# Output projection: half 0 left open in eight banks, mix loaded into its final places, factors loaded ahead of values

## The chip, the cores and the metric

One core of a Trainium2 chip runs the whole program. The metric is device time in microseconds (us), the median of the runs shown below. Every matrix product works on numbers split in two (a rounded high part and the rest), so that one fp32 product takes three matmuls: high x high, high x low, low x high.

## The reference

One layer of a hybrid decoder: for a prompt of 2048 rows and 32 sample rows, of width 1024. Cut to what matters here:

```python
def _layer_prompt(x, biases, ...):
    q, k, v, u, vg = _project(x, norm1_g, w_in)          # rmsnorm(x) @ w_in
    for (w, d), bias_hj in zip(BRANCHES, biases):        # (128,1), (512,4), (2048,16)
        o, l = _dilated_prompt(q, k, v, bias_hj, d, w // d + 1)
        outs.append(o); lses.append(l)
    att = _merge_branches(outs, lses)                    # softmax over the branches' lse
    gate = _spatial_gate(vn, sgu_w, sgu_b)
    x = x + jnp.concatenate([att, u * gate], axis=-1) @ w_out
    return x + _swiglu(x, norm2_g, w_gate, w_up, w_down)
```

The product with `w_out` (1024 x 1024) is the output projection, and its left operand is called mix here: 512 columns of attention (8 heads of 64) and 512 of the gating unit.

## The kernel before

**Stages.** Projection of the input and the gating unit come first; then attention, head by head; then, for each of two blocks of 1024 rows, output projection, norm, gate and up products, down products and the final norm. Block 0 is rows 0 to 1023 in 8 tiles of 128. Block 1 is the other 8 tiles and the sample rows.

**Attention.** Each of 8 heads is 20 items of softmax work. A planner holds the code: `at(step, phase, fn)` puts a function at a step (one item, about 2.2 us) and a phase of it, and the code of each engine is written in that order. `L` is the step of the last item and `U0` is `L + 7`, where attention's last pieces end. The branches of a head are merged with factors: `weights_store` (L957) writes them from ACT's queue to `f_d` in DRAM, `merge_load` reads them back, spread over partitions, `merge` multiplies and adds in three operations on POOL or DVE, and `merge_store` writes a head pair's attention columns to `cat_d` in DRAM, where mix lies transposed. Attention's rows lie there in two parts that are added later. Heads are worked in pairs; a slice of mix is 128 of its 1024 columns, and slice s = 7 holds heads 6 and 7, the last to be ready. Merges of a head run during the next head's items; those of head 7 are left for the output projection.

**Output projection.** A unit is one tile of 128 rows by one half of 512 output columns: 8 slices x 3 matmuls into one bank (`out_unit`, L1255 to L1257), followed by an add of the bank to `acc`, which holds x. `load_cat` brings a tile of mix from `cat_d` to a staging tile `fr` (two buffers, used by the weights' `load_wo` too) and the second part of attention to `raw`. `split_cat` adds the two on DVE, copies the sum to the high part `xh` on ACT (L122) and subtracts for the low part `xl` on DVE (L125). A weight goes through `fr` likewise: ACT makes `woh` or `wol` from it, POOL subtracts. All these loads, x (`acc`), factors of head 7 and stores of its merges share SP's queue, which issues in order and waits where an entry must wait.

**Order in block 0.** At steps U0 to U0+7, units of half 0 run without slice 7 (21 matmuls each), are added to `acc`, and head 7 is merged meanwhile: factors from step U0+2 on, chunk by chunk of 512 rows. `last_load` (L1401) and `last_split` bring slice 7. From step U0+8 on, each step holds a whole unit of half 1 and slice 7 of a half 0 unit (3 matmuls), which is added to `acc` in turn. Unit 0 takes its mix from `pair` tiles filled in attention's last steps.

**Order in block 1.** A plain loop: tile i+1 is split ahead of unit i, tile i+3 is loaded, and the weights of half 1 are loaded at tiles 1 to 4.

Of the kernel before, what the change touches and what calls it, by code (L numbers as in the profile page):

```python
# [10 lines left out]
F32 = mybir.dt.float32  # L11
# [8 lines left out]
P = 128  # L20
# [44 lines left out]
def hymba_step(ctx: ExitStack, tc: tile.TileContext, A: dict, O: dict):  # L65
# [896 lines left out]
    def merge_load(h, ch):  # L962
        if h < H - 1:
            f = pair_tile(F32)
            mf[h, ch] = (f[:, 0], f[:, 1])
            act.dma_start(f, dap(f_d, h * 2 * T + ch * 512, [[0, P], [T, 2], [1, 512]]))
# [145 lines left out]
    def fraw():  # L1112
        return pool_["fw"].tile([P, 1024], F32, name="fr", tag="fr", bufs=2)

    def fminor():
        return raw_tile()

# [72 lines left out]
    def load_acc(B, i):  # L1190
        if B.rows[i] == P:
            B.acc[i] = fc.tile([P, D], F32, name="acc%d" % i, tag="acc%d" % i)
# [22 lines left out]


    def load_cat(B, i, ns, staged=None):
        t0 = (B.b0 + i) * P
        if staged is None:
            r = fraw().rearrange("p (s t) -> p s t", s=KD)  # L1220
            parts = (r[:, 0:4], r[:, 4:8])
            m = fminor().rearrange("p (s t) -> p s t", s=4)
        else:
            r = None
            *parts, m = (x.rearrange("p (s t) -> p s t", s=4) for x in staged)
        na = ns - 4
        raws["c", B.b0 + i] = (r, parts, m)
        for dst, r0, n in ((parts[0], 0, 4), (parts[1], DA, na), (m, D, na)) if staged else ((r, 0, ns), (m, D, na)):
            sync.dma_start(dst[:, 0:n], cat_d[r0:r0 + n * P, t0:t0 + P].rearrange("(s p) t -> p s t", p=P))

    def split_cat(B, i, ns, place, eng=dve):
        r, parts, m = raws.pop(("c", B.b0 + i))
        ch, cl = B.cat[i] = place
        na = ns - 4
        eng.tensor_add(parts[1][:, 0:na], parts[1][:, 0:na], m[:, 0:na])
        if r is not None:
            split_sb(ch[:, 0:ns], cl[:, 0:ns], r[:, 0:ns], eng_lo=eng)
        else:
            split_sb(ch[:, 0:4], cl[:, 0:4], parts[0], eng_lo=eng)
            split_sb(ch[:, 4:ns], cl[:, 4:ns], parts[1][:, 0:na], eng_lo=eng)  # L1240

    def place_of(B, i):

        return B.xh[:, :, i * P:(i + 1) * P], B.xl[:, :, i * P:(i + 1) * P]

    def out_unit(B, i, half, ss=range(KD)):
        tick()
        hs = slice(half * 512, (half + 1) * 512)
        ps = ps_o()
        for s in ss:  # L1250
            first, last = s == ss[0], s == ss[-1]
            wh, wl = B.wo[half, s]
            if B.rows[i] == P:
                ch, cl = (x[:, s, :] for x in B.cat[i])
                pe.matmul(ps, ch, wh, start=first, stop=False)  # L1255
                pe.matmul(ps, ch, wl, start=False, stop=False)  # L1256
                pe.matmul(ps, cl, wh, start=False, stop=last)  # L1257
            else:
                c = cats[:, (s + 4) % KD, :]
                pe.matmul(ps[0:2 * SR], c, wh, start=first, stop=False)  # L1260
                pe.matmul(ps[0:2 * SR], c, wl, start=False, stop=last)
        if B.rows[i] == P:
            dve.tensor_add(B.acc[i][:, hs], B.acc[i][:, hs], ps)
        else:
            tmp = zn_tile()[0:SR]
            act.activation(tmp, ps[SR:2 * SR, :], AF.Copy)
            dve.tensor_add(B.acc[i][0:SR, hs], B.acc[i][0:SR, hs], ps[0:SR])
            dve.tensor_add(B.acc[i][0:SR, hs], B.acc[i][0:SR, hs], tmp)

    def rms_b(s1, n):  # L1270
# [123 lines left out]

    last = {}

    def last_load(ch):

        x, m = last[ch] = (fraw(), None)
        for z, r0 in enumerate((DA + 3 * P, D + 3 * P)):  # L1400
            sync.dma_start(x[:, z * 512:(z + 1) * 512], cat_d[r0:r0 + P, ch * 512:(ch + 1) * 512])  # L1401

    def last_split(ch):
        x = last.pop(ch)[0]
        dve.tensor_add(x[:, 0:512], x[:, 0:512], x[:, 512:1024])
        if ch == 0:
            ch_, cl_ = B.cat[0]
            split_sb(ch_[:, 7], cl_[:, 7], x[:, 0:P], eng_lo=dve)
            split_sb(B.xh[:, 7, P:512], B.xl[:, 7, P:512], x[:, P:512], eng_lo=dve)
        else:  # L1410
            split_sb(B.xh[:, 7, 512:1024], B.xl[:, 7, 512:1024], x[:, 0:512], eng_lo=dve)

# [21 lines left out]
    B.xl = fc.tile([P, KD, TB], F32R, name="xl2", tag="xl2")  # L1434
    for i in range(1, 3):
        load_cat(B, i, 7)
    for i in range(2):
        load_acc(B, i)
    for nm in ("norm2_g", "final_g"):
        gain.append(row_tile(nm))  # L1440
    for i in range(1, 8):
        at(U0 + i - 1, "early", lambda i=i: split_cat(B, i, 7, place_of(B, i)))
        if i + 2 < 8:
            at(U0 + i - 1, "early", load_cat, B, i + 2, 7)
        if i > 1:
            at(U0 + i - 2, "misc", load_acc, B, i)
    h = H - 1
    for ch, s, eng in ((0, 3, dve), (1, 3, pool), (2, 5, dve), (3, 5, pool)):
        at(U0 + s - 1, "misc", merge_load, h, ch)
        at(U0 + s, "misc", merge, h, ch, eng)  # L1450
        at(U0 + s + 1, "misc", merge_store, h, ch, ch + 1)
    at(U0 + 6, "misc", lambda: [sync.dma_start(g_, dap(A[nm], 0, [[0, P], [1, D]])) for g_, nm in zip(gain, ("norm2_g", "final_g"))])
    for ch in range(2):
        at(U0 + 7 + ch, "misc", last_load, ch)
        at(U0 + 8 + ch, "early", last_split, ch)
    for s2, s, e in ((0, 3, 4), (1, 4, 5), (2, 5, 6), (3, 6, 7)):
        at(U0 + s, "misc", load_wo, B, 1, s2, fraw)
        at(U0 + e, "misc", half1_split, B, s2)
    for i in range(8):
        at(U0 + i, "values", out_unit, B, i, 0, range(7))  # L1460
        at(U0 + 8 + i, "values", out_unit, B, i, 1)
        at(U0 + 8 + i, "values", out_unit, B, i, 0, (7,))
        at(U0 + 8 + i, "out", lambda i=i: later(1, norm2_a, B, i))
    at(U0 + 10, "misc", load_gate, 0)
    at(U0 + 12, "misc", split_gate, 0)
    plan.run(10 ** 9)

    for bi, B in enumerate(blocks):
        if bi:
            for i in range(B.nt):  # L1470
                if i + 1 < B.nt:
                    split_cat(B, i + 1, 8, place_of(B, i + 1))
                if i + 3 < B.nt:
                    load_cat(B, i + 3, 8)
                elif i + 3 < B.nt + 2:
                    pass
                out_unit(B, i, 0)
# [20 lines left out]
        for f in range(NF):  # L1498
# [32 lines left out]
            if f % FC == FC - 1:  # L1531
# [4 lines left out]
                elif end:  # L1536
                    nb.xh = fc.tile([P, KD, TB], F32R, name="xh2", tag="xh2")
                    nb.xl = fc.tile([P, KD, TB], F32R, name="xl2", tag="xl2")
                    for n, fn, args in ((1, load_wo, (nb, 0, 2, fraw)), (1, load_cat, (nb, 0, 8)),
                                        (3, split_wo, (nb, 0, 2, gate_tiles, dve)), (3, load_wo, (nb, 0, 3, fraw)),  # L1540
                                        (4, split_cat, (nb, 0, 8, place_of(nb, 0))), (4, load_cat, (nb, 1, 8)),
                                        (5, split_wo, (nb, 0, 3, gate_tiles, dve)), (5, load_cat, (nb, 2, 8))):
                        later(n, fn, *args)
# [113 lines left out]
```

## Time and profile before

| | us |
|---|---|
| median of 3 runs | 2867.06 (2865.78 to 2869.12) |
| the profiled execution | 2874.03 |
| its span, first to last instruction | 2872.2 |
| block 0's output projection, first matmul to the first of the gate | 1059.31 to 1184.51 |
| block 1's, first matmul to the end of half 1's first unit | 1934.45 to 2013.66 |

The mean granted TensorE clock was 0.963 of full. The page cuts the span into 40 equal slices of 71.8 us, and each digit is the busy share of TensorE in one, in tenths:

```profile
PE   8988897988998987999999999997999999999997
```

Block 0's output projection lies in slices 15 to 17 (8, 7, 9), block 1's in 27 to 29 (9, 7, 9). Under a row of a timeline, the bracket holds the idle time just before the instruction and what ended it. "SPq" and "ACTq" are DMA issues.

### The profile page before, as it was taken

What the parts mean: (1) busy time and instruction counts of PE and PEld (TensorE: products, weight loads), DVE (VectorE), ACT (ScalarE), POOL (GpSimd) and SP (SyncE); (2) the same over time, 40 slices, a digit from 0 to 9 for tenths busy, and PEclk for the clock granted to TensorE, in tenths of its full rate; (3) what the DMA queues carried; (4) which work ended last, traced back from release to release, by engine and by line L of the source; (5) the groups of instructions that cost most, each with busy time, mean ns of one, the idle gap of its engine ahead of it and who ended that gap; (6) DMA issues with size and microseconds to landing.
All of it is one profiled execution on the core that took longest, in us unless ns stands there. A gap on an engine that the chain in (4) does not pass through costs nothing.

```text
span 2872.2 us, 33608 instructions
## 1 busy us (share of the span) xinstructions
PE 2680.6 (93%) x13058; PEld 2260.2 (79%) x13058; DVE 1197.0 (42%) x2287; ACT 762.5 (27%) x1426; POOL 849.5 (30%) x558
## 2 busy tenths in 40 slices
PE   8988897988998987999999999997999999999997
PEld 6776675667888875888888888875799999999996
DVE  3257775335677764522222222244522222222224
ACT  5413233435676751310100000021300000000002
POOL 1034742121243442232232222211132222222222
PEclk9999998999899988999999999998999999999999
DMA  8654933676556556232223222235132222222211
GB/s 243 206 176 128 283 105 111 185 217 227 154 174 197 150 163 189 88 112 93 88 89 110 95 88 88 95 107 181 54 108 88 88 88 88 88 88 88 89 44 61
DMA packets 285940, 367.44 MB, mean 128 GB/s; under 512 B 18487, under 2 KB 214248, under 8 KB 279764
## 3 DMA queue, kind: packets, MB, share of 16 engines
q1 hardware_dynamic: 270868, 341.56, 37.2%
q10 hardware_dynamic: 14912, 23.73, 3.3%
q8 instruction: 103, 1.69, 0.3%
q14 instruction: 57, 0.47, 0.1%
HBM read 309.88 MB, written 125.47 MB: 152 GB/s over the span
## 4 chain that ended last, share of the span: by engine, by line
PE 71%; DVE 8%; DMA 6%; ACT 4%; issue 4%; POOL 2%; SPq 1%; ACTq 0%; POOLq 0%; DVEq 0%
PE ps_o L1341 17%; PE ps_s L1315 12%; PE ps_s L1316 12%; PE ps_s L1317 12%; PE ps_s L295 2%; PE ps_s L296 2%; PE ps_s L297 2%; DVE pl L847 1%; PE ps_o L1255 1%; PE ps_o L1257 1%; PE ps_o L1256 1%; PE ps_s L810 1%; DMA fr<-in_w_out_dram 1%; PE ps_o L861 1%; PE ps_t L838 1%
## 5 line engine op out<-in xcount | busy, mean ns | idle before, releaser
L1315 PE MATMUL ps_s<-xh,gh 128*128 128x352 f32 (+1 forms) x1760 | 624.1, 355 | 0.0
L1317 PE MATMUL ps_s<-xh,gl 128*128 128x352 f32 (+1 forms) x1760 | 620.2, 352 | 0.0
L1316 PE MATMUL ps_s<-xl,gh 128*128 128x352 f32 (+1 forms) x1760 | 619.5, 352 | 0.0
L1341 PE MATMUL ps_o<-dw,hw 128*128 128x512 f32 x2112 | 499.8, 397 | 9.7 <-DVE acc L1343 9.7
L1341 PEld LDWEIGHTS ps_o<-dw,hw 128*128 128x128 f32 x2112 | 395.6, 188 | 109.0 <-DVE acc L1343 15.6
L1319 ACT ACTIVATE zn<-ps_s 128x352 f32<-128x352 f32 (+1 forms) x110 | 57.1, 519 | 1319.0 <-PE ps_s L1317 1319.0
L1320 DVE TENSOR_TENSOR zn<-zn,ps_s 128x352 f32<-128x352 f32 (+1 forms) x110 | 64.6, 587 | 721.5 <-ACT zn L1319 721.5
L1315 PEld LDWEIGHTS ps_s<-xh,gh 128*128 128x128 f32 x1760 | 332.3, 189 | 33.5
L1316 PEld LDWEIGHTS ps_s<-xl,gh 128*128 128x128 f32 x1760 | 331.3, 188 | 31.6
L1317 PEld LDWEIGHTS ps_s<-xh,gl 128*128 128x128 f32 x1760 | 330.4, 188 | 32.4
L1343 DVE TENSOR_TENSOR acc<-acc,ps_o 128x512 f32<-128x512 f32 x352 | 241.1, 687 | 214.4 <-PE ps_o L1341 214.4
L125 POOL TENSOR_TENSOR hw<-zn,hw 128x512 fp32r<-128x512 f32 (+2 forms) x110 | 119.8, 1089 | 661.1 <-DVE hw L124 592.9
L125 POOL TENSOR_TENSOR gl<-fr,gh 128x1024 fp32r<-128x1024 f32 x88 | 212.8, 2442 | 130.3 <-ACT gh L122 130.3
L125 POOL TENSOR_TENSOR dw<-fr,dw 128x1024 fp32r<-128x1024 f32 x44 | 106.7, 2424 | 378.8 <-DVE dw L124 378.8
L295 PE MATMUL ps_s<-wh,xh 128*128 128x512 f32 x480 | 200.9, 419 | 6.5 <-ACT xh L122 6.1
L296 PE MATMUL ps_s<-wl,xh 128*128 128x512 f32 x480 | 195.4, 407 | 6.7 <-DVE wl L207 6.7
L297 PE MATMUL ps_s<-wh,xl 128*128 128x512 f32 x480 | 195.3, 407 | 0.0
L295 PEld LDWEIGHTS ps_s<-wh,xh 128*128 128x128 f32 x480 | 94.6, 197 | 38.2 <-issue 9.7
L296 PEld LDWEIGHTS ps_s<-wl,xh 128*128 128x128 f32 x480 | 94.7, 197 | 26.1 <-DVE wl L207 8.3
L297 PEld LDWEIGHTS ps_s<-wh,xl 128*128 128x128 f32 x480 | 94.4, 197 | 21.3 <-DVE xl L125 0.2
L821 ACT ACTIVATE e<-e,st 128x640 f32<-128x640 f32 (+4 forms) x128 | 96.3, 752 | 2.1 <-DVE st L816 2.0
L816 DVE CUSTOM_DVE_ANT_0 e<-ps_s,b 128x640 f32<-128x640 f32 (+4 forms) x128 | 93.4, 730 | 3.8 <-PE ps_s L810 3.8
(325 smaller groups left out, 4064.2 us busy)
## 6 DMA issues: line engine op xcount, KB each, us to landing
out_ks_dram<-in_cache_k_dram SPq DMA_DIRECT2D x56, 512.0 KB
out_vs_dram<-in_cache_v_dram SPq DMA_DIRECT2D x56, 512.0 KB
fr<-in_w_gate_dram SPq DMA_DIRECT2D x44, 512.0 KB
fr<-in_w_up_dram SPq DMA_DIRECT2D x44, 512.0 KB
fr<-in_w_down_dram SPq DMA_DIRECT2D x44, 512.0 KB
raw<-in_w_in_dram SPq DMA_DIRECT2D x72, 256.0 KB
qk_d<-pair SPq DMA_DIRECT2D x64, 256.0 KB
pair<-f_d ACTq DMA_DIRECT2D x28, 512.0 KB
```

The costliest lines, as they stand in the source:

```text
L125: (eng_lo or pool).tensor_sub(lo, src, hi.bitcast(F32))
L295: pe.matmul(o[j], xh[:, k, :], wh, start=(k == 0), stop=False)
L296: pe.matmul(o[j], xh[:, k, :], wl, start=False, stop=False)
L297: pe.matmul(o[j], xl[:, k, :], wh, start=False, stop=(k == KD - 1))
L816: dve.tensor_tensor_reduce(e[:, 0:w], s[:, c0:c0 + w], d["b12"][:, 640 - w:640], 1.0, BIG, OP.add, OP.min, st[:, 0, n:n + 1])
L821: act.activation(e[:, 0:w], e[:, 0:w], AF.Exp, bias=st[:, 0, n:n + 1], scale=-1.0, accum_out=st[:, 1, n:n + 1])
L1315: pe.matmul(ps[:, q_, 0:n], wh[:, ks], B.xh[:, k, a:b], start=(k == 0), stop=False)
L1316: pe.matmul(ps[:, q_, 0:n], wh[:, ks], B.xl[:, k, a:b], start=False, stop=False)
L1317: pe.matmul(ps[:, q_, 0:n], wl[:, ks], B.xh[:, k, a:b], start=False, stop=(k == KD - 1))
L1320: dve.tensor_mul(sg[:, 0:n], sg[:, 0:n], ps[:, 1, 0:n])
L1341: pe.matmul(ps[0:nr], l_, r_[:, cs], start=(z == 0 and y == 0), stop=(z == FC - 1 and y == len(ops) - 1))
L1343: dve.tensor_add(B.acc[i][0:nr, cs], B.acc[i][0:nr, cs], ps[0:nr])
```

## The change

Five things change together.

- **Half 0 of block 0 stays open.** Eight banks hold the eight accumulations (two tiles `ps_s` of two banks and four single banks). `open_unit` runs slices 0 to 6, and `close_unit` runs slice 7 into the same bank later and adds it to `acc` once. `last_load` and `last_split` are made for all of block 0's rows at once. The closes go ahead of half 1's units: tiles 4, 5, 0 ahead of the first, then 1, 2, 3, and 6 with 7.
- **Unit 0 moves into attention's last steps**, L+2 to L+6, with its mix loaded at L-3 and split at L+1.
- **Mix goes to its final places.** `load_cat` writes the tile of mix into `xl` and the second part of attention into `xh`, without `fr`. `split_cat` adds them into a small tile, and makes the high and low parts in place: one add, two copies on ACT, two subtracts on DVE. In block 1 all tiles are loaded during block 0's last down units.
- **Head 7's factors** are loaded from step U0 on, ahead of the mix of tiles 3 to 7; its chunks 0 and 1 (block 0's rows) are stored at U0+2, the others at U0+3.
- **In attention**, each head's factors are loaded at step 8 of the next head instead of 11 (ahead of the values of the head after, loaded at 10 and 12 instead of 13 and 15); merges and stores move by three and two steps.

```diff
     def merge_load(h, ch):
-        if h < H - 1:
+        if h < H - 2 or h == H - 2 and ch < 2:
...
-        for y in (1, 2, 3, 4, 13, 15):
+        for y in (1, 2, 3, 4, 10, 12):
             at(s0 + y, "misc", load, h)
...
-            for ch, (a, b) in enumerate(((11, 13), (11, 16), (16, 19), (19, 22))):
+            for ch, (a, b) in enumerate(((8, 11), (8, 14), (14, 17), (17, 20))):
...
-            at(s0 + 25, "store", merge_store, h, 0, 4)
+            at(s0 + 23, "store", merge_store, h, 0, 4)
...
+    def load_cat(B, i, ns, place=None):
+        ch, cl = B.cat[i] = place or place_of(B, i)
+        for dst, r0, n in ((cl[:, 0:ns], 0, ns), (ch[:, 4:ns], D, ns - 4)):
+            sync.dma_start(dst.bitcast(F32), cat_d[r0:r0 + n * P, t0:t0 + P].rearrange("(s p) t -> p s t", p=P))
+
+    def split_cat(B, i, ns, staged=raw_tile):
+        ch, cl = B.cat[i]
+        m = staged()[:, 0:(ns - 4) * P].rearrange("p (s t) -> p s t", t=P)
+        dve.tensor_add(m, cl[:, 4:ns].bitcast(F32), ch[:, 4:ns].bitcast(F32))
+        for a, b, x in ((0, 4, cl[:, 0:4].bitcast(F32)), (4, ns, m)):
+            act.activation(ch[:, a:b], x, AF.Copy)
+            dve.tensor_sub(cl[:, a:b], x, ch[:, a:b].bitcast(F32))
...
+    def open_unit(i, ss=range(KD - 1)):
+        if ss[0] == 0:
+            open_bank(i)
+        out_part(B, i, 0, ss, open_[i], ss[0] == 0, False)
+
+    def close_unit(i):
+        out_part(B, i, 0, (KD - 1,), open_[i], False, True)
+        out_end(B, i, 0, open_.pop(i))
+
+    def last_load():
+
+        for dst, r0 in ((B.xl, DA + 3 * P), (B.xh, D + 3 * P)):
+            sync.dma_start(dst[:, 7, 0:8 * P].bitcast(F32), cat_d[r0:r0 + P, 0:8 * P])
+
+    def last_split():
+        for c in range(2):
+            xh, xl = (x[:, 7, c * 512:(c + 1) * 512] for x in (B.xh, B.xl))
+            m = late_acc(c)
+            dve.tensor_add(m, xl.bitcast(F32), xh.bitcast(F32))
+            act.activation(xh, m, AF.Copy)
+            dve.tensor_sub(xl, m, xh.bitcast(F32))
...
-    at(L + 1, "misc", lambda: load_cat(B, 0, 7, (raw_tile(), raw_tile(), zn_tile())))
-    at(L + 4, "misc", lambda: split_cat(B, 0, 7, first_place()))
+    at(L - 3, "misc", lambda: load_cat(B, 0, 7, first_place()))
+    at(L + 1, "misc", split_cat, B, 0, 7)
+    for j, ss in enumerate(((0, 1), (2,), (3,), (4, 5), (6,))):
+        at(L + 2 + j, "misc", open_unit, 0, ss)
...
+    at(U0, "early", loads_now, (load_cat, B, 1, 7), (load_cat, B, 2, 7), (merge_load, h, 0), (merge_load, h, 1), (load_cat, B, 3, 7),
+       (merge_load, h, 2), (load_cat, B, 4, 7))
     for i in range(1, 8):
-        at(U0 + i - 1, "early", lambda i=i: split_cat(B, i, 7, place_of(B, i)))
-        if i + 2 < 8:
-            at(U0 + i - 1, "early", load_cat, B, i + 2, 7)
...
+        at(U0 + i - 1, "low", split_cat, B, i, 7, lambda i=i: late_acc(i))
+        at(U0 + i - 1, "values", open_unit, i)
+    at(U0 + 1, "misc", merge, h, 1, pool)
+    at(U0 + 2, "exp", merge, h, 0, dve)
+    at(U0 + 2, "misc", loads_now, (merge_store, h, 0, 2), (merge_load, h, 3), (load_cat, B, 5, 7), (last_load,),
+       (load_cat, B, 6, 7), (load_cat, B, 7, 7), (load_acc, B, 4), (load_acc, B, 5), (load_wo, B, 1, 0, fraw), (load_wo, B, 1, 1, fraw))
...
+    at(U0 + 5, "misc", half1_split, B, 0)
+    at(U0 + 6, "exp", half1_split, B, 1)
+    at(U0 + 6, "exp", loads_now, (load_wo, B, 1, 2, fraw), (load_wo, B, 1, 3, fraw), (load_acc, B, 2), (load_acc, B, 3))
+    at(U0 + 6, "misc", last_split)
...
+    for j, shut in enumerate(((4, 5, 0), (1,), (2,), (3,), (6, 7), (), (), ())):
+        for i in shut:
+            at(U0 + 7 + j, "values", close_unit, i)
+        at(U0 + 7 + j, "values", out_unit, B, j, 1)
...
     for bi, B in enumerate(blocks):
         if bi:
             for i in range(B.nt):
                 if i + 1 < B.nt:
-                    split_cat(B, i + 1, 8, place_of(B, i + 1))
-                if i + 3 < B.nt:
-                    load_cat(B, i + 3, 8)
...
+                    split_cat(B, i + 1, 8)
                 out_unit(B, i, 0)
                 if i in (1, 2, 3, 4):
                     load_wo(B, 1, i - 1, fraw)
...
+                                        (4, split_cat, (nb, 0, 8)), (5, split_wo, (nb, 0, 3, gate_tiles, dve))] + [
+                                            (i + 1, load_cat, (nb, i, 8)) for i in range(2, nb.nt)]:
                         later(n, fn, *args)
```

Three places show the new order. Names carry a buffer number; `cat_d` is mix in DRAM, `f_d` the factors, and what stands in brackets are the semaphores that an entry waits for. First SP's queue in block 0's half 0, before: x, the factors of chunks 0 and 1, then the mix of tiles 5 and 6 and the first weight.

```order
L1194 DMA acc4_9909<-in_x_prompt_dram 128x1024
L970 DMA raw_9911<-f_d_66 128x512 [waits DMAHW4_49]
L970 DMA zn_9912<-f_d_66 128x512 [waits DMAHW5_49]
L970 DMA raw_9915<-f_d_66 128x512 [waits DMAHW7_49,DMAHW6_49,DVE_49]
L970 DMA zn_9916<-f_d_66 128x512
L1229 DMA fr_9922<-cat_d_65 128x7x128 [waits DMAHW0_49,DVE_49]
L1229 DMA raw_9923<-cat_d_65 128x3x128 [waits DMAHW4_49,DMAHW1_49,DVE_49]
L1194 DMA acc5_9949<-in_x_prompt_dram 128x1024 [waits DMAHW2_49]
L1207 DMA fr_9957<-in_w_out_dram 128x2x512 [waits DMAHW3_49,DVE_49]
L1229 DMA fr_9962<-cat_d_65 128x7x128 [waits DMAHW3_49,Pool_49]
L1229 DMA raw_9963<-cat_d_65 128x3x128 [waits DMAHW6_49,DMAHW5_49]
L1194 DMA acc6_9989<-in_x_prompt_dram 128x1024
```

And of the change, from the mix of tile 2 on:

```order
L1225 DMA xl2_9812<-cat_d_65 128x7x128 [waits DMAHW0_49]
L1225 DMA xh2_9811<-cat_d_65 128x3x128 [waits DMAHW1_49]
L971 DMA raw_9820<-f_d_66 128x512 [waits DMAHW5_49,DMAHW2_49]
L971 DMA zn_9821<-f_d_66 128x512 [waits DMAHW3_49]
L971 DMA raw_9824<-f_d_66 128x512 [waits DMAHW4_49]
L971 DMA zn_9825<-f_d_66 128x512
L1225 DMA xl2_9812<-cat_d_65 128x7x128 [waits DMAHW6_49]
L1225 DMA xh2_9811<-cat_d_65 128x3x128 [waits DMAHW7_49]
L971 DMA raw_9830<-f_d_66 128x512 [waits DMAHW0_49]
L971 DMA zn_9831<-f_d_66 128x512 [waits DMAHW1_49]
L1225 DMA xl2_9812<-cat_d_65 128x7x128 [waits DMAHW2_49]
L1225 DMA xh2_9811<-cat_d_65 128x3x128 [waits DMAHW3_49]
```

The factors of chunks 0 to 2 moved from behind the mix of tile 4 to behind that of tile 2, x and the weights went behind all mix, and the stores of chunks 0 and 1 stand ahead of tile 5. Next ACT at the end of block 0's half 0, before:

```order
L122 ACTIVATE xh2_9788<-fr_9882 128x7x128 [waits DMAHW1_49,DVE_49]
L122 ACTIVATE woh_10003<-fr_9957 128x1024 [waits DMAHW3_49,Pool_49]
L122 ACTIVATE xh2_9788<-fr_9922 128x7x128 [waits DMAHW0_49,DVE_49]
L122 ACTIVATE wol_10042<-fr_10006 128x1024 [waits DMAHW7_49,DMAHW2_49]
L122 ACTIVATE xh2_9788<-fr_9962 128x7x128 [waits DMAHW4_49,DVE_49]
L122 ACTIVATE woh_10079<-fr_10045 128x1024 [waits DMAHW1_49,Activation_49,Pool_49]
L122 ACTIVATE wol_10110<-fr_10082 128x1024 [waits DMAHW4_49,DMAHW3_49,DMAHW5_49,DMAHW2_49,DMAHW0_49]
```

And of the change, where `xh2` from `acc6` or `acc7` is the attention part of a split, and L1422 is slice 7:

```order
L1232 ACTIVATE xh2_9811<-xl2_9812 128x4x128 [waits DMAHW4_49]
L1232 ACTIVATE xh2_9811<-acc7_9873 128x3x128 [waits DMAHW5_49,DVE_49]
L122 ACTIVATE woh_10049<-fr_9952 128x1024 [waits DMAHW2_49,Pool_49]
L122 ACTIVATE wol_10052<-fr_9954 128x1024 [waits DMAHW3_49]
L1232 ACTIVATE xh2_9811<-xl2_9812 128x4x128 [waits DMAHW6_49]
L1232 ACTIVATE xh2_9811<-acc7_9873 128x3x128 [waits DMAHW7_49,DVE_49]
L1422 ACTIVATE xh2_9811<-acc6_9836 128x512 [waits DVE_49] x2
L122 ACTIVATE woh_10097<-fr_10055 128x1024 [waits DMAHW0_49,Activation_49,Pool_49]
L122 ACTIVATE wol_10100<-fr_10057 128x1024 [waits DMAHW5_49,DMAHW4_49,DMAHW1_49]
```

A split is now two copies. The first two weights stand ahead of the copies of one tile instead of alternating with three of them. Last, SP's queue in block 1's half 0, before, with a weight, a tile of mix, a store of the output and a tile of x in turn:

```order
L1207 DMA fr_15008<-in_w_out_dram 128x2x512 [waits DMAHW2_49,DVE_49]
L1229 DMA fr_15013<-cat_d_65 128x8x128 [waits DMAHW3_49,DMAHW2_49,Pool_49]
L1229 DMA raw_15014<-cat_d_65 128x4x128
L1371 DMA out_yp_dram<-acc6_9989 128x1024 [waits DMAHW5_49]
L1194 DMA acc5_15023<-in_x_prompt_dram 128x1024 [waits DMAHW6_49,DMAHW0_49]
L1207 DMA fr_15051<-in_w_out_dram 128x2x512 [waits DMAHW7_49,DVE_49]
L1229 DMA fr_15059<-cat_d_65 128x8x128 [waits DMAHW7_49,Pool_49]
L1229 DMA raw_15060<-cat_d_65 128x4x128 [waits DMAHW1_49]
```

And of the change, at the end of block 0's down units, where these tiles of mix now stand:

```order
L1206 DMA fr_14669<-in_w_out_dram 128x2x512 [waits DMAHW4_49,DVE_49]
L1225 DMA xl2_14668<-cat_d_65 128x8x128 [waits DMAHW7_49,PE_49]
L1225 DMA xh2_14667<-cat_d_65 128x4x128 [waits PE_49]
L1225 DMA xl2_14668<-cat_d_65 128x8x128 [waits DMAHW1_49]
L1225 DMA xh2_14667<-cat_d_65 128x4x128
L1206 DMA fr_14714<-in_w_out_dram 128x2x512 [waits DMAHW5_49,DMAHW3_49,DVE_49]
L1225 DMA xl2_14668<-cat_d_65 128x8x128
L1225 DMA xh2_14667<-cat_d_65 128x4x128
L1225 DMA xl2_14668<-cat_d_65 128x8x128 [waits DMAHW6_49]
L1225 DMA xh2_14667<-cat_d_65 128x4x128 [waits DMAHW7_49]
```

The mix of all tiles stands around the last weight of half 0 there, goes into `xl2` and `xh2`, and no entry of it waits for a staging buffer's reader (DVE or POOL).

More of the change, by code (lines that the diff above doesn't have):

```diff
@@ L1191, in load_acc @@
         if B.rows[i] == P:
-            B.acc[i] = fc.tile([P, D], F32, name="acc%d" % i, tag="acc%d" % i)
+            if i not in B.acc:
+                B.acc[i] = fc.tile([P, D], F32, name="acc%d" % i, tag="acc%d" % i)
             t0 = (B.b0 + i) * P
@@ L1250, in out_unit, with out_part @@
+    def split_cat(B, i, ns, staged=raw_tile):
[5 more added lines that the diff above has]
+            dve.tensor_sub(cl[:, a:b], x, ch[:, a:b].bitcast(F32))
+    def out_part(B, i, half, ss, ps, start, stop):
         for s in ss:
-            first, last = s == ss[0], s == ss[-1]
+            first, last = start and s == ss[0], stop and s == ss[-1]
@@ L1261, in out_unit, with out_end @@
                 pe.matmul(ps[0:2 * SR], c, wl, start=False, stop=last)
+    def out_end(B, i, half, ps):
+        hs = slice(half * 512, (half + 1) * 512)
         if B.rows[i] == P:
@@ L1268, in out_unit @@
             dve.tensor_add(B.acc[i][0:SR, hs], B.acc[i][0:SR, hs], tmp)
+    def out_unit(B, i, half):
+        tick()
+        ps = ps_o()
+        out_part(B, i, half, range(KD), ps, True, True)
+        out_end(B, i, half, ps)
     def rms_b(s1, n):
@@ L1393, in first_place, with open_bank, late_acc @@
         return tuple(pair_tile().rearrange("p a b -> p (a b)").rearrange("p (s t) -> p s t", s=KD) for _ in range(2))
[L1395 to L1409, printed above, removed]
-        else:
-            split_sb(B.xh[:, 7, 512:1024], B.xl[:, 7, 512:1024], x[:, 0:512], eng_lo=dve)
+    open_ = {}
+    def open_bank(i):
+        if i in (0, 1, 6, 7):
+            if i % 2 == 0:
+                open_["s"] = ps_s()
+            open_[i] = open_["s"][:, i % 2]
+        else:
+            open_[i] = bank(i - 2)
+    def open_unit(i, ss=range(KD - 1)):
[15 more added lines that the diff above has]
+            dve.tensor_sub(xl, m, xh.bitcast(F32))
+    def late_acc(n):
+        i = 6 + n % 4 // 2
+        if i not in B.acc:
+            B.acc[i] = fc.tile([P, D], F32, name="acc%d" % i, tag="acc%d" % i)
+        return B.acc[i][:, n % 2 * 512:(n % 2 + 1) * 512]
     stage = {}
@@ L1447, in hymba_step @@
[L1447 to L1465, printed above, removed]
+    h = H - 1
```

57 lines of the change are left out of this document (16 added, 41 removed).

## The prediction

> **What bounds the kernel now.** I read the page's chain of waits first, then a table of stretches.
>
> ```profile
> PE 71%; DVE 8%; DMA 6%; ACT 4%; issue 4%; POOL 2%; SPq 1%; ACTq 0%; POOLq 0%; DVEq 0%
> ```
>
> The chain lies on TensorE for 71%; the other 29% is what can be won without fewer matmuls. The table has, by stretch, its length, then busy time and count of PE, weight loads, DVE, ACT and POOL, the granted clock, the DMA share and GB/s. The rows are block 0's output projection up to the first gate matmul, its last third, the FFN, and block 1's first half.
>
> ```profile
> 1059.31:1184.51 125.20, 104.43 (x435) 81.25 (x435) 60.02 (x95) 31.58 (x50) 24.31 (x12) 0.90 0.53 164
> ...
> 1140.00:1184.51 44.51, 44.19 (x216) 35.96 (x215) 28.96 (x60) 16.30 (x32) 5.75 (x2) 1.00 0.19 63
> ...
> 1200.00:1890.00 690.00, 690.00 (x2960) 554.76 (x2959) 173.54 (x267) 63.51 (x82) 203.09 (x104) 1.00 0.28 94
> 1934.45:2013.66 79.21, 63.19 (x233) 47.87 (x234) 31.92 (x43) 13.77 (x18) 9.47 (x4) 0.87 0.53 177
> ```
>
> The FFN is bound by PE (690.00 of 690.00 busy): nothing to win. The two projection stretches are not. The price of one matmul comes from PE's timeline:
>
> ```profile
> 1071.09 0.40 PE L1257 MATMUL ps_o<-gh,xl 128*128 128x512 f32 x1
> ...
> 1087.78 0.40 PE L1257 MATMUL ps_o<-gh,xl 128*128 128x512 f32 x1
> ```
>
> These two are 72 matmuls (three units) apart: 16.69 / 72 = 0.2318 us each. Block 0 has 8 tiles x 2 halves x 8 slices x 3 = 384 matmuls, 89.0 us. Six groups of norm transposes also lie ahead of the gate:
>
> ```profile
> 1147.02 0.87 PE ps_t L1299 x8
> ```
>
> that is 5.2 us. So 125.2 - 89.0 - 5.2 = **31.0 us lost in block 0**. Block 1's stretch holds 8 x 24 matmuls, 16 for the sample rows and 24 of the first unit of half 1: 232 x 0.2318 = 53.8 of 79.2, **25.4 us lost in block 1**. Who is waited for (total us, times, longest), first block 0, then block 1:
>
> ```profile
> PE ps_o L1255 <- ACT xh L122: 11.9, 3, 10.2
> PE ps_o L1257 <- DVE xl L125: 3.6, 3, 1.8
> ...
> PE ps_o L1255 <- ACT xh L122: 9.9, 3, 4.6
> PE ps_o L1257 <- DVE xl L125: 6.1, 4, 1.8
> ```
>
> Both wait for the split of mix, and ACT, which makes it, waits in order. Its timeline around the longest wait of block 0, and its waits over block 1's stretch:
>
> ```profile
> 1112.50 1.06 ACT L122 ACTIVATE wol<-fr 128x1024 fp32r<-128x1024 f32 x1 [16.84 <-DMA fr<-in_w_out_dram]
> 1113.46 0.93 ACT L122 ACTIVATE xh<-fr 128x896 fp32r<-128x896 f32 x1
> ...
> ACT wol L122 <- DMA fr<-in_w_out_dram: 21.3, 2, 10.8
> ACT woh L122 <- DMA fr<-in_w_out_dram: 16.0, 2, 10.6
> ```
>
> The copy of mix stood behind a weight copy that waited 16.84 us for its DMA. The chain shows why those DMAs are late: factor, weight and mix loads follow one another on SP and through the two staging buffers.
>
> ```profile
> 1078.45 7.02 DMA raw<-f_d
> ...
> 1103.76 7.33 DMA zn<-f_d
> ...
> 1123.93 4.58 DMA fr<-cat_d
> 1128.71 2.57 DVE fr L1405
> ...
> 1959.48 6.83 DMA fr<-in_w_out_dram
> ```
>
> **The change, block 0.** The matmuls stay 384, but 21 of them (unit 0, seven slices) go among the attention's last steps, whose stretch is:
>
> ```profile
> 1045.00:1059.31 14.31, 11.30 (x51) 9.77 (x51) 7.34 (x19) 7.60 (x16) 8.89 (x8) 0.64 0.45 106
> ```
>
> 21 x 0.2318 = 4.9 us, against 14.31 - 11.30 = 3.0 us idle. At best 1.9 is added. At worst they run at half clock, 21 x 0.42 = 8.8 (rows below), and 5.8 is added. I take 2.7, near the lower end, since denser work there should raise the 0.64: the tail ends at 1062.0 instead of 1059.3.
>
> Then PE waits. Mix of tile 1 goes into memory that attention frees, so its load starts at the tail's end, as the first load did before, and what it released came 7.4 us later:
>
> ```profile
> 1059.44 0.37 SPq L1229 DMA_DIRECT2D fr<-cat_d  x1
> ...
> 1066.88 0.64 PE L1255 MATMUL ps_o<-gh,xh 128*128 128x512 f32 x1 [2.47 <-ACT o L917]
> ```
>
> Before, unit 0 filled most of that. Now nothing does: 7.4 us idle, 4.8 if the load needn't wait for the last attention matmul. After an idle time the clock is low:
>
> ```profile
> 1098.26 0.79 PE L1257 MATMUL ps_o<-gh,xl 128*128 128x512 f32 x1 [1.82 <-DVE xl L125]
> ...
> 1114.45 0.79 PE L1255 MATMUL ps_o<-gh,xh 128*128 128x512 f32 x1 [10.19 <-ACT xh L122]
> ...
> 1118.11 0.63 PE L1256 MATMUL ps_o<-gl,xh 128*128 128x512 f32 x1
> 1118.53 0.63 PE L1257 MATMUL ps_o<-gh,xl 128*128 128x512 f32 x1
> ```
>
> The last two start 0.42 apart; about ten such matmuls cost 10 x 0.2 = 2.0 us. Units 1 to 6 then run from 1062.0 + 7.4 + 2.0 = 1071.4 without a stop if each split takes less than a unit, 21 x 0.2318 = 4.87 us. The split's operations:
>
> ```profile
> 1064.21 0.56 DVE L1235 TENSOR_TENSOR fr<-fr,raw 128x384 f32<-128x384 f32 x1 [6.94 <-DMA raw<-cat_d]
> 1065.92 1.09 DVE L125 TENSOR_TENSOR xl<-fr,xh 128x896 fp32r<-128x896 f32 x1 [1.15 <-ACT xh L122]
> ...
> 1094.90 2.36 POOL L125 TENSOR_TENSOR woh<-fr,woh 128x1024 fp32r<-128x1024 f32 x1 [2.02 <-ACT woh L122]
> 1095.69 2.52 DVE L125 TENSOR_TENSOR xl<-fr,xh 128x896 fp32r<-128x896 f32 x1 [3.96 <-ACT xh L122]
> ```
>
> On DVE 0.56 + 1.09, at worst 0.56 + 2.52 = 3.1, and ACT's two copies (some 1.1) lie beside: covered, so I price it at 0, like DVE's eight additions of partial sums that fall away. Were the splits not ahead of PE, the seven would cost 7 x 1.65 = 11.6. The Trainium skill ("SBUF — State Buffer", section "Who interferes with whom") says that a DVE instruction with two SBUF inputs contends with a GpSimd instruction that reads SBUF. That speaks against head 7's merges on POOL beside the splits; the 2.52 beside POOL's subtract, against 1.09, agrees. If the cover did not hold, an estimate by it adds the difference for two units, 2.9 us (2829).
>
> What comes last in half 0 is unit 7: its copies stand in ACT's order behind the first two weight factors of half 1, the two behind the merged mix of head 7 on SP. Up to there the queue carries seven tiles of mix at 640 KB, four factor chunks and two stores (2.5 MB), head 7's rows (1 MB), two tiles of x (1 MB) and two factors (1 MB): 10.1 MB. A full DMA's rate, and the first and last of the three operations of a merge on POOL:
>
> ```profile
> 1080.00:1090.00 10.00, 8.91 (x38) 6.59 (x36) 5.24 (x7) 1.57 (x2) 2.32 (x2) 1.00 1.00 285
> ...
> 1087.68 1.51 POOL L977 TENSOR_TENSOR ob<-ob,raw 128x512 f32<-128x512 f32 x1 [33.63 <-DMA raw<-f_d]
> ...
> 1091.39 1.49 POOL L981 TENSOR_TENSOR ob<-ob,o 128x512 f32<-128x512 f32 x1
> ```
>
> At 285 GB/s that is 35.4 us from 1062.0. With 2.6 for SP's waits for the merges (an estimate: half of one merge of 1092.9 - 1087.7 = 5.2) the factors land at 1100. Unit 7 is due at 1071.4 + 6 x 4.87 = 1100.6 and starts, after two weight copies and its own split, at 1102.3: 1.7 lost, and 2.0 of half clock. The Trainium skill ("TensorE: Matmul & The Clock Gate", section "What's actually happening") halves the clock only after an idle window of about 3.4 us. The row at 1098.26, after waits of under 2 us, already took 0.79, so I keep the 2.0. By the rule the sum would be 2824.
>
> Then the eight closes, 24 matmuls, and half 1 run through, with 1.0 for anything else. Sum: 1062.0 + 363 x 0.2318 (84.1) + 5.2 + 7.4 + 2.0 + 1.7 + 2.0 + 1.0 = 1165.4, against 1184.5: **-19**. Bounds: -25 (tail at its best, only the first wait and its clock left) to -10 (tail +3.1, and one more factor landing of about 6 us on the way).
>
> **Block 1.** The eight mix loads stand ahead of the weights of half 1 on SP and don't need `fr`; they land during block 0's last down units. What is left for ACT to wait for is four weights of 512 KB, now alone, with half 0's 208 matmuls (48.2 us) as cover; before, one took 6.83. At 285 GB/s one takes 1.8. I leave 1.5 of 25.4: **-24**. Bounds: -25 to -16, one wait of 7.2 left with its half clock.
>
> **Attention.** A head's factors are read back two steps (4.5 us) after they are stored, five steps before, on ACT's queue:
>
> ```profile
> 966.60 0.37 ACTq L957 DMA_DIRECT2D f_d<-f  x1
> ...
> 978.26 0.37 ACTq L966 DMA_DIRECT2D pair<-f_d  x1
> ...
> 1011.24 0.37 ACTq L957 DMA_DIRECT2D f_d<-f  x1
> ...
> q10 hardware_dynamic: 272, 0.02, 4.5%
> ```
>
> (11.66 us, five steps.) The last row is the stretch 1013 to 1017, which holds the small packets of the second store: up to 5.8 us to land, so the load can hold ACT 1.3 us, with the scores' exp behind it and PE behind that. Seven heads: 0 to 12, if each is paid in full with some dispatch. I take +2: the other store landed within 2 us, and PE has work queued. The values' loads, POOL's merges and the stores move two or three steps earlier with the same bytes and operations; I price them at 0, since POOL is idle 70% of the span (row below), and a load of values that lands early only waits for its head.
>
> ```profile
> PE 2680.6 (93%) x13058; PEld 2260.2 (79%) x13058; DVE 1197.0 (42%) x2287; ACT 762.5 (27%) x1426; POOL 849.5 (30%) x558
> ```
>
> **The sum**: -19 - 24 + 2 = -41. On the profiled execution, 2874.0 - 41 = 2833; it stands 7.0 above the median of 2867.06, so the median goes to **2826**. With the bounds: -50 to -14, 2817 to 2853.
>
> **The rivals.**
>
> *The chain of factors keeps block 0 (0.12).* Head 7's factors, merges and stores took 7.02 and 7.33 us apiece on the chain; if the last split still comes at 1131.3 (1128.71 + 2.57), eight closes, 5.6, half 1, 44.5, transposes, 5.2, and 2 of clock follow it: 1188.6, 4 later. With block 1's -24 and +2: 2849. Against it: the loads are issued ahead of most of mix, not behind it.
>
> *Block 1's copies still wait behind the weights in ACT's order (0.12).* The order of ACT is not changed there: the 10.8 us wait for a weight remains if the landing is bound by something other than mix. Then only -19 + 2 remain: 2850. For it: the queue before had 6.83 for 512 KB, four times the price at 285 GB/s. Against it: outputs and mix shared that queue.
>
> *Slower (0.05).* ACT's queue stops at the factor load until the store has landed, in seven heads. The cover is 4.5 us; the other terms bring -43, so it decides from 4.5 + 43 / 7 = 10.6 us to land. If it took 13 us, (13 - 4.5) x 7 = 59.5, +16.5: 2883. The rows show at most 5.8, against it.
>
> *It does not do what it says (0.05).* PE waits for bytes, not for order: the stretch of block 0 moved 125.2 us x 164 GB/s = 20.5 MB, 72 us at 285, and what is won early is lost at the weights and at the gate's first factors; block 1 likewise. Then about 2867. Against it: DMA shares of 0.53 in both.
>
> **How the numbers follow.** The forecast holds 0.66: 2826. The first two rivals, 2849 and 2850, lie in the range that the bounds give; I widen it by 1 to 2 us for the attention's unknown order: 2815 to 2854. The last two rivals, 0.10, are left out with the tails. 0.2% is 5.7 us, about what a measurement can tell from no change. Faster: 0.66 + 0.12 + 0.12 = 0.90; same 0.05; slower 0.05.
>
> **What would show it.** Half 0's first matmul on tile 1 some 7 us behind the last attention matmul, at half clock; PE then without gaps for six units; the gate's first matmul at 1165, moved by what attention costs. In block 1, no wait of PE for the split above 2 us and a stretch of 55 us instead of 79. In attention, ACT waiting for the factors' store by under 2 us a head. It is wrong if unit 7 or the closes wait for the merged mix, or if ACT's waits for weights in block 1 stay at 10 us.

## The result and the profile after

| | before | after |
|---|---|---|
| median, us | 2866.42 (4 runs, 2865.35 to 2869.12) | 2802.87 (4 runs, 2801.76 to 2803.51) |
| the profiled execution, us | 2874.03 | 2803.45 |
| its span, us | 2872.2 | 2801.7 |

The ratio is 0.9776, 95% interval 0.976 to 0.9793: 63.6 us faster. Forecast were 41, with a range of 2815 to 2854; the time lies 12 us below the range. Of all executions in this document one, 3287.98 us at a granted clock of 0.741, was in a slow state, and the times leave it out. The slices of TensorE and the chain, as the page of the changed kernel has them:

```profile
PE   8988897988999989999999999999999999999997
...
PE 73%; DVE 9%; DMA 6%; ACT 3%; issue 3%; POOL 1%; SPq 1%; ACTq 0%; DVEq 0%; POOLq 0%
```

The 7 of slice 16 and the 7 of slice 28 are gone, and TensorE's share of the chain went from 71 to 73%. But slice 13, in attention, rose as well, from 8 to 9; there the prediction had 2 us lost. The stages, with the same columns as before (length first, busy PE second, clock third from the end); first the kernel before, head 6's store of factors to the last attention matmul:

```profile
1011.24:1059.31 48.07, 41.86 (x240) 37.43 (x239) 32.97 (x77) 33.91 (x73) 27.61 (x19) 0.86 0.55 142
```

The same stretch of the changed kernel, then from there to the gate, and block 1's stretch:

```profile
983.46:1036.82 53.36, 48.45 (x260) 42.75 (x259) 34.94 (x77) 33.83 (x73) 28.61 (x19) 0.84 0.40 112
...
1036.82:1140.19 103.37, 94.35 (x406) 74.82 (x406) 48.91 (x83) 28.99 (x50) 27.25 (x15) 0.93 0.63 197
1889.58:1943.00 53.42, 53.42 (x232) 42.58 (x233) 29.71 (x50) 14.67 (x25) 9.62 (x4) 1.00 0.59 200
```

Block 1 lost 25.4 us before and loses nothing now: 53.42 of 53.42 busy. Block 0 from the tail's end to the gate takes 103.37, against 125.20. The tail, from head 6's store to the end of attention's matmuls, grew by 53.36 - 48.07 = 5.3. Together these are near the forecast. The new part is ahead of it: head 6's store comes at 983.46 instead of 1011.24, 27.8 us earlier. What PE waits for in these two stages of the changed kernel (us, times, longest), block 0, then block 1:

```profile
PE ps_s L1242 <- ACT xh L1232: 8.1, 2, 4.7
PE ps_s L1242 <- DVE acc L1253: 0.8, 1, 0.8
...
PE ps_o L1242 <- DVE acc L1339: 0.3, 1, 0.3
```

So the question is where attention's gain comes from. The same head in both profiles, from its store of factors to the next one's, before and after:

```profile
824.35:871.49 47.14, 42.57 (x268) 39.39 (x267) 33.98 (x86) 32.15 (x77) 18.60 (x17) 0.92 0.65 188
```

```profile
809.54:852.11 42.57, 40.62 (x268) 36.98 (x268) 34.95 (x88) 32.86 (x79) 19.27 (x16) 1.00 0.67 207
```

The same 268 matmuls take 4.6 us less: PE is idle 2.0 instead of 4.6 us, and its clock is 1.00 instead of 0.92. At the end of that head, four timelines of the kernel before (ACT's queue, POOL, ACT, PE) read one after another:

```profile
855.02 0.37 ACTq L966 DMA_DIRECT2D pair<-f_d  x1
...
867.24 1.29 POOL L977 TENSOR_TENSOR ob<-ob,pair 128x512 f32<-128x512 f32 x1 [6.96 <-DVE f L953]
868.49 1.04 POOL L886 TENSOR_TENSOR e<-e,st 128x512 f32<-128x512 f32 x1
...
869.56 0.63 ACT L889 ACTIVATE e<-e 128x512 f32<-128x512 f32 x1 [3.73 <-POOL e L886]
...
870.24 0.66 PE L898 MATMUL ps_t<-ident,e 128*128 128x128 f32 x4 [2.53 <-ACT e L889]
```

The load of the factors of chunk 3, the last of a head, is issued at 855.02. POOL starts the merge that needs it at 867.24, after 6.96 us idle; behind it in POOL's order stands the subtract of a strided item (L886), behind that ACT's exp (L889), behind that PE's transposes (L898). The releaser that the bracket names, a reciprocal on DVE, has nothing to do with that merge: it only came last. One head earlier the bracket in the same place names the load itself:

```profile
819.52 1.26 POOL L977 TENSOR_TENSOR ob<-ob,pair 128x512 f32<-128x512 f32 x1 [7.50 <-DMA pair<-f_d]
```

Why the load took so long shows on SP's queue, around the moment of its issue, and in the stretch between issue and use:

```profile
854.07 0.56 SPq L773 DMA_DIRECT2D qh<-qk_d  x1
854.72 0.56 SPq L773 DMA_DIRECT2D k<-qk_d  x1
855.33 0.60 SPq L773 DMA_DIRECT2D ql<-qk_d  x1
```

```profile
855.00:867.20 12.20, 11.65 (x79) 10.75 (x78) 9.84 (x33) 7.74 (x21) 5.19 (x5) 1.00 0.93 331
```

The DMA engines are 0.93 busy: the next head's q and k (three loads of 1 MB) went out at the same time, and 0.5 MB of factors took 12 us among them. In the changed kernel the load goes out ahead of them, and its merge doesn't wait:

```profile
834.95 0.37 ACTq L967 DMA_DIRECT2D pair<-f_d  x1
...
841.17 1.28 POOL L978 TENSOR_TENSOR ob<-ob,pair 128x512 f32<-128x512 f32 x1
```

That is theory A: factors that land late hold POOL, and POOL holds the scores of the strided item behind them. Over six heads (729 to 1012) the waits of PE for L889 in the kernel before are

```profile
PE ps_t L898 <- ACT e L889: 8.9, 3, 3.3
...
PE ps_o L898 <- ACT e L889: 4.9, 2, 3.0
```

13.8 us, and the low clock (0.92 over these heads) comes on top. Its rival B: values were late, and moving their loads is the gain.

### The profile page after: what moved, and what is told of

Its sections match the earlier page's. It is cut to its first block, busy times and chain, and to the rows that moved or that the text cites. A ratio compares the mean times of both kernels' runs of the same rounds, so it can differ in the third digit from the quotient of the medians.

```text
span 2801.7 us, 33627 instructions
## 1 busy us (share of the span) xinstructions
PE 2658.8 (95%) x13058; PEld 2244.4 (80%) x13058; DVE 1193.9 (43%) x2290; ACT 763.3 (27%) x1440; POOL 851.8 (30%) x561
## 4 chain that ended last, share of the span: by engine, by line
PE 73%; DVE 9%; DMA 6%; ACT 3%; issue 3%; POOL 1%; SPq 1%; ACTq 0%; DVEq 0%; POOLq 0%
PE ps_o L1337 17%; PE ps_s L1311 12%; PE ps_s L1312 12%; PE ps_s L1313 12%; DVE pl L847 2%; PE ps_o L1242 2%; PE ps_o L1244 2%; PE ps_o L1243 2%; PE ps_o L861 2%; PE ps_s L295 2%; PE ps_s L296 1%; PE ps_s L297 1%; PE ps_s L810 1%; DVE e L816 1%; DMA kv<-zs_d 1%
## 5 line engine op out<-in xcount | busy, mean ns | idle before, releaser
L297 PEld LDWEIGHTS ps_s<-wh,xl 128*128 128x128 f32 x480 | 94.6, 197 | 21.3 <-DVE xl L125 0.2
```

The costliest lines, as they stand in the source:

```text
L297: pe.matmul(o[j], xl[:, k, :], wh, start=False, stop=(k == KD - 1))
```

## The experiments

The first six are the kernel before with a part of attention's schedule, the others the changed kernel with a part put back or moved. Each was timed beside the kernel before on the same chip, and the ratio is to that: its median was 2867.44 beside the first four, 2868.15 beside the next four, 2870.24 and 2868.85 beside the last two pairs.

**All of attention's schedule, nothing else.**

```diff
-        for y in (1, 2, 3, 4, 13, 15):
+        for y in (1, 2, 3, 4, 10, 12):
...
-            for ch, (a, b) in enumerate(((11, 13), (11, 16), (16, 19), (19, 22))):
+            for ch, (a, b) in enumerate(((8, 11), (8, 14), (14, 17), (17, 20))):
...
-            at(s0 + 25, "store", merge_store, h, 0, 4)
+            at(s0 + 23, "store", merge_store, h, 0, 4)
```

> The kernel before with only attention's schedule of the change (factors at steps 8, 8, 14, 17, merges at 11, 14, 17, 20, store at 23, values at 10 and 12). If the part of the gain that was not foreseen lies in this schedule, the profiled heads give 27.8 us up to head 6's store, less up to 7 since the profiled execution of before stood 7 us above its median: 2838 to 2846. If it comes from an interplay with the new output projection: 2860 or more.

Measured 2847.78, ratio 0.9933 (0.9918 to 0.9948), -19.7 by the medians. Attention brings that by itself; the time is 1.8 above the expected 2838 to 2846. The 27.8 of the profiles is too much because attention took longer than usual in the profiled execution of before: in the profiles of three other kernels that load and merge chunk 3 as before (values only, chunk 3 as before, the projection alone; all below), head 6's store comes at 1003 to 1007, not at 1011.

**Factors, merges and store early, values left; and the reverse.**

```diff
-            for ch, (a, b) in enumerate(((11, 13), (11, 16), (16, 19), (19, 22))):
+            for ch, (a, b) in enumerate(((8, 11), (8, 14), (14, 17), (17, 20))):
...
-            at(s0 + 25, "store", merge_store, h, 0, 4)
+            at(s0 + 23, "store", merge_store, h, 0, 4)
```

> The kernel before with factors, merges and store three, three and two steps earlier, values left at 13 and 15. Theory A (on POOL the subtract of a strided item stands behind the first operation of chunk 3's merge, which waits for factors that land 12 us after their issue, behind the next head's q and k): nearly all of attention's gain is here, 2840 to 2850. Theory B (values land too late for the matmuls that use them, and the move from 13 and 15 to 10 and 12 is the gain): 2862 or more.

```diff
-        for y in (1, 2, 3, 4, 13, 15):
+        for y in (1, 2, 3, 4, 10, 12):
```

> The kernel before with the loads of values at steps 10 and 12, factors and merges left. Theory A: 0 or a loss, 2860 to 2880, as the values now go ahead of the factors on the DMA engines. Theory B: 2838 to 2850.

Measured 2849.88 (0.9937, 0.9923 to 0.9952) for the merges and 2867.73 (1.0001, 0.9991 to 1.0012) for the values. Theory B falls: the gain goes with the merges (factor loads, merges and the store at 23), -17.6 of -19.7, and the values' loads alone bring nothing.

**The merge of chunk 3 one step later.**

```diff
-            for ch, (a, b) in enumerate(((11, 13), (11, 16), (16, 19), (19, 22))):
+            for ch, (a, b) in enumerate(((11, 13), (11, 16), (16, 19), (19, 23))):
...
-            at(s0 + 25, "store", merge_store, h, 0, 4)
+            at(s0 + 26, "store", merge_store, h, 0, 4)
```

> The kernel before with the merge of chunk 3 one step LATER (23 to 25 in place of 22 to 24, store at 26), no load moved: its first operation then stands behind the strided subtract on POOL, not ahead of it. Theory A: most of the gain, 2842 to 2855. Theory B, or that factors and merges must come early for any other reason: 2862 to 2872.

Measured 2859.11 (0.9974, 0.9959 to 0.9989): -8.3, under half of the gain and outside both expectations. In its profiled execution (2865.37, the second longest of its ten and 6.3 above their median) PE no longer waits for L889 at all, but other waits came up, for the scores behind the strided ones and, on ACT, for the store that now ends later:

```profile
PE ps_s L877 <- DVE st L816: 4.1, 3, 2.4
...
ACT ob L870 <- DMA cat_d<-ob: 4.6, 2, 2.9
```

The order on POOL is part of it; this run alone couldn't say how large. The next two separate the landing from the place.

**Chunk 3 loaded early and merged at its old place; and chunk 3 as before with the others early.**

```diff
-            for ch, (a, b) in enumerate(((11, 13), (11, 16), (16, 19), (19, 22))):
+            for ch, (a, b) in enumerate(((8, 11), (8, 14), (14, 17), (17, 22))):
```

> The kernel before with factors at 8, 8, 14, 17, merges at 11, 14, 17 and chunk 3's at its old steps 22 to 24, store at 25, values left. Chunk 3's first operation stands ahead of the strided subtract on POOL as before, but its factors have landed. Theory A (the late landing is what holds the subtract): 2846 to 2853, as with all merges early. Theory C (the place on POOL costs by itself, each operation ahead of the subtract delaying it): 2858 to 2867.

```diff
-            for ch, (a, b) in enumerate(((11, 13), (11, 16), (16, 19), (19, 22))):
+            for ch, (a, b) in enumerate(((8, 11), (8, 14), (14, 17), (19, 22))):
```

> The kernel before with chunks 0 to 2 early (loads 8, 8, 14, merges 11, 14, 17) and chunk 3 left as before (load 19, merge 22 to 24, store 25). Theory A: the factors land late again behind q and k of the next head, so 2860 to 2868. If it is the earlier chunks that bring the gain: 2846 to 2853.

Measured 2852.47 (0.9945, 0.993 to 0.996) and 2870.19 (1.0009, 0.9998 to 1.002). The two differ in one number, the step of one load per head, 17 or 19, and by 17.7 us. PE's waits over six heads in the second:

```profile
PE ps_t L898 <- ACT e L889: 8.7, 3, 3.2
...
PE ps_o L898 <- ACT e L889: 4.9, 2, 3.0
```

13.6 us as before, and none of it in the first, whose merge stands at its old place ahead of the subtract; the clock over these heads is 0.99 in the first and 0.94 in the second. So it is the late landing of chunk 3's factors that held POOL. The place alone costs little: 2852.47 is 2.6 above the run with all merges early, with overlapping intervals. The other three chunks bring nothing.

**The projection alone**: the changed kernel with attention's schedule put back, the first diff reversed.

> The changed kernel with attention's schedule put back (factors at 11, 11, 16, 19, merges at 13, 16, 19, 22, store at 25, values at 13 and 15). The prediction's terms without attention's: 2867 - 43 = 2824. If attention's 20 us and the rest add: 2803 + 20 = 2823. If the new output projection had itself gained more than was priced: 2812 or less.

Measured 2824.93 (0.9846, 0.983 to 0.9862): -43.2, where the prediction's terms give -43. The two parts add: -19.7 - 43.2 = -62.9, against 63.6.

**Block 1's mix loaded in the loop again**, into its final places.

```diff
-                                            (i + 1, load_cat, (nb, i, 8)) for i in range(2, nb.nt)]:
+                                            (i + 1, load_cat, (nb, i, 8)) for i in range(2, 3)]:
...
                     split_cat(B, i + 1, 8)
+                if i + 3 < B.nt:
+                    load_cat(B, i + 3, 8)
```

> The changed kernel with block 1's mix of tiles 3 to 8 loaded in the loop again, tile i+3 at tile i, between the weights of half 1 on SP, still into their final places. If the shared staging buffers were what made block 1 wait: at most 3 us lost, 2803 to 2806, and no wait of PE over 2 us in block 1. If it was mix between the weights on the queue: 10 to 25 us lost, 2813 to 2828.

Measured 2803.91 (0.9771, 0.9755 to 0.9788; the change itself 0.9776). ACT's waits for weights in its block 1:

```profile
ACT woh L122 <- DMA fr<-in_w_out_dram: 2.5, 2, 1.6
ACT wol L122 <- DMA fr<-in_w_out_dram: 2.3, 2, 1.5
```

4.8 us instead of 37.3 (21.3 + 16.0), although mix and weights alternate on SP again, and PE waits for none of it. So the order on the queue was not the cause. What is left of the change there is that mix no longer goes through the two shared buffers, where a load of mix had to wait for the weight before it to be split, and the next weight for the mix; undoing that by itself was not tried.

**Unit 0 out of attention's last steps.** The tail had grown by 5.3 us, and PE waits 4.7 us right behind it.

```diff
-    for j, ss in enumerate(((0, 1), (2,), (3,), (4, 5), (6,))):
-        at(L + 2 + j, "misc", open_unit, 0, ss)
...
+    at(U0, "exp", open_unit, 0)
```

> The changed kernel with all of unit 0's seven slices behind attention's last matmul instead of among its last steps (mix still loaded and split early). The tail should lose the 5.3 us that it grew by (48.1 from head 6's store to the last attention matmul, not 53.4), and the 4.7 us wait for tile 1's mix is filled with 21 matmuls. Theory D (in the tail they cost their full price, as PE is at half clock there): faster than the change by 2 to 5 us, 2798 to 2801. Theory E (they filled idle time in the tail, as predicted, and only move): 2802 to 2805.

> The changed kernel with slices 0 to 2 of unit 0 among attention's last steps and 3 to 6 behind its last matmul: 12 matmuls, 2.8 us at full clock or 5.0 at half, into the wait of 4.7. Theory D: between the change and the run with all seven behind, 2799 to 2802, or best of the three if the slices of the first two steps lie in idle time. Theory E: 2802 to 2804.

(The second leaves slices 0 to 2 at L+2 and L+3.) Measured 2805.56 (0.9778, 0.9762 to 0.9793) and 2808.05 (0.9789, 0.9773 to 0.9805). Neither did what it was for: the last attention matmuls stand in a later phase of step U0, so unit 0 still ran ahead of them, and the wait was 4.70 and 4.71. They say only that these places in the tail are worth about the same. The next two runs take the same slices, in the second 2 to 6, to another phase: with `"values"` in place of `"exp"` they stand behind those matmuls.

> The changed kernel with all of unit 0's seven slices behind the last attention matmul, in the wait for tile 1's mix (in the two runs before they still stood ahead of that matmul, and the wait stayed 4.7 us). Theory D: the loads of mix, which are released by the last attention matmul, start 3 to 5 us earlier, the wait is filled, and the gate's first matmul comes 3 to 5 us earlier after head 6's store: 152 to 154 us instead of 156.7; 2798 to 2801. Theory E (half 0 ends where the merged mix and the weights land, whatever PE does ahead of that): 156 to 157 us, 2802 to 2805.

> The changed kernel with slices 0 and 1 of unit 0 at step L+2, where PE waits 3.0 us otherwise, and slices 2 to 6 behind the last attention matmul: 15 matmuls, 3.5 us, in the wait of 4.7. Theory D: as good as all seven behind, or 1 to 2 us better: 151 to 154 us from head 6's store to the gate, 2797 to 2801. Theory E: 156 to 157 us, 2802 to 2805.

Measured 2801.2 (0.976, 0.9744 to 0.9775) and 2804.05 (0.9777, 0.9763 to 0.979). In the first's profile, head 6's store to the last attention matmul, and from there to the gate:

```profile
983.64:1034.64 51.00, 42.13 (x240) 37.57 (x238) 34.62 (x77) 33.62 (x73) 28.60 (x19) 0.87 0.43 117
1034.64:1137.60 102.96, 97.46 (x428) 77.32 (x427) 49.24 (x83) 29.00 (x50) 27.75 (x15) 0.97 0.62 198
```

153.96 instead of 156.73, 2.8 us less, as theory D has it (156.38 in the run with block 1's loads in the loop, which has the change's code there). In the second's profile it is 155.02, between what D and E expected. The times can't tell either from the change: the intervals overlap. The wait of 4.7 is filled, but PE catches up with the same weights of half 1 and waits 3.7 there.

## Why the prediction missed

**The failed step** is attention: "POOL's merges and the stores move two or three steps earlier with the same bytes and operations; I price them at 0, since POOL is idle 70% of the span", and with it the bounds "0 to 12", which left no room for a gain. The earlier factor loads were priced only for the wait for their store, at +2; when they land, and what stands behind their merge on POOL, was not asked. An idle share over the span says nothing on an engine whose order holds another's work: POOL was idle because its next operation waited for factors, with the subtract of the scores behind it. In place of +2 the runs show -19.7, and -17.7 by the step of chunk 3's load alone. Nothing was quoted of attention's own waits; a table of one head gives PE 4.6 us idle and clock 0.92, and the waits for L889 show there by name. With -20 for that term the sum is -63, where 63.6 was measured.

**Block 0 was right in its steps and near in its sum.** From head 6's store to the gate it gained 173.27 - 156.73 = 16.5, where 19 was forecast. These rows are SP, PE and ACT of the changed kernel:

```profile
1037.13 0.38 SPq L1225 DMA_DIRECT2D xl<-cat_d  x1
...
1041.82 0.80 PE L1242 MATMUL ps_s<-gh,xh 128*128 128x512 f32 x1 [4.72 <-ACT xh L1232]
...
1074.08 1.06 ACT L122 ACTIVATE woh<-fr 128x1024 fp32r<-128x1024 f32 x1 [5.30 <-DMA fr<-in_w_out_dram]
...
1076.96 0.80 PE L1242 MATMUL ps_s<-gh,xh 128*128 128x512 f32 x1 [3.42 <-ACT xh L1232]
```

- The mix of tile 1 is loaded right behind the last attention matmul (1036.82), as worked out, but the wait is 4.72, not 7.4: the copy of the four slices that need no add starts when the first of the two loads has landed. The 4.8 that the prediction named is near it for another reason: it supposed a load ahead of the last matmul.
- The first weight of half 1 is ready 37.0 us after that first load (1074.08 - 1037.13); 38 were forecast. Unit 7 waits behind the weights in ACT's order, as forecast, 3.42 instead of 1.7.
- From the tail's end to the gate it is 103.37, where 1165.4 - 1062.0 = 103.4 was worked out. That they agree is luck: the two misses above, -2.7 and +1.7, cancel with a third, the half clock behind unit 7's wait, 3.0 where 2.0 was taken (the 13 matmuls from 1076.96 to 1083.01 took 6.05 us, at 0.2318 each 3.0).
- The price of 0.2318 holds, though its 72 matmuls are not three units (a unit of half 0 has 21), and so does 38 us for the loads; but 285 GB/s is not the most that the DMA engines move, as the row of attention with 331 at a share of 0.93 shows.
- Unit 0 in the tail costs 2.4 (53.36 against 51.00 with it behind the last matmul), where 2.7 was taken. But the tail grew by more, to 53.36 from 47.95 (both to the start of the last attention matmul), and the shares don't add: 49.96 with attention's schedule alone, 52.98 with the projection alone. What goes beyond unit 0 had no term, and its cause stays open.

**Block 1 was right**: -24 forecast, 25.4 in the profile (126.7 to 101.3 from first matmul to the gate), with no wait for the split left. The reason was named in two halves, the place ahead of the weights on SP and that `fr` isn't needed; the run with the loads back in the loop shows that the first isn't needed.

**The rivals** fell: head 7's merged mix was not late for the closes, the weights did not hold block 1, and bytes did not bound either stretch. The slower one, ACT's queue held by the factors' store, did not come to pass: no wait for that store is on PE's or ACT's list over attention in the changed kernel, and the early loads gain.

**The weighed rules.** The splits beside POOL's merges took up to 1.78 us for a subtract of 0.68, as the Trainium skill ("SBUF — State Buffer", section "Who interferes with whom") would have it; PE waited for none of units 2 to 6, so the cover held. The other rule is the Trainium skill's idle window of about 3.4 us ahead of the half clock ("TensorE: Matmul & The Clock Gate", section "What's actually happening"). The half clock after unit 7's wait can't decide on it: 3.42 us is just that window.

The sum that the prediction made against the profiled execution carried a second trap: that execution was 7.0 us above its median, and 4 to 8 us lay in attention by the profiles of the other kernels (head 6's store at 1011, against 1003 to 1007), the stage that was not looked at.

## What to carry to other kernels

Take a table of one period of every long stage, also of one that the change only brushes: idle time of the bottleneck and its clock there show what is to be won before the reason is known. When a load is moved, ask for what is queued behind its reader on the reader's own engine: a side job on an otherwise idle engine, a merge here, sets the pace of the main work as soon as its data come late and main work stands behind it. A staging buffer that two streams share can make each wait for the other's consumers; here that is the cause that is left when the order of the loads is ruled out, not one that was tried by itself.

## What was not expected of the hardware

A load of 512 KB takes 12.2 us from issue to its first use when 3 MB for another reader go out within a microsecond of it (855.02 to 867.24, DMA share 0.93), and under 6.3 us when it goes out a few us ahead of them (834.95 to 841.17). In the first case 37 of its 272 packets moved in the first 5 us (to 860), 149 in the next 4 and 86 after that: the small transfer was served among the large ones, not ahead of them. The kernel before varies more from execution to execution than three runs show: 2859.89 to 2874.58 over 19, against 2865.78 to 2869.12 over the first three.
